# Small DMAs issued by GpSimd, and the SSD group norm spread as rows through DRAM

## The chip, the cores and the metric

One core of a Trainium2 chip runs the whole program. The metric is the device time of one execution in microseconds; lower is better. The core has five engines with a queue of instructions each: TensorE (PE), VectorE (DVE), ScalarE (ACT), GpSimd (POOL) and SyncE (SP). An engine takes its queue in order; semaphores tie the queues together.

## The reference

A decoder trunk of two layers on x of 512 tokens by 1024 channels, in float32. Each layer:

```python
u = rmsnorm(h); proj = u @ w_in              # D_IN columns for three branches and the gates
y_gla = group_rmsnorm(gla(q, k, v, decay), 4 groups) * silu(gg)
y_m   = group_rmsnorm(mlstm(q, k, v, i, f), 4 groups) * sigmoid(mo)
y = ssd(x, dt, a, b, c) + d * x              # 16 heads in 2 groups, chunked scan
y = y * silu(sz)
y_s   = group_rmsnorm(y, ssd_norm, 2 groups) # mean of squares over 512 channels, per token
z = [y_gla, y_m, y_s] @ w_branch             # one 1024 x 1024 product each
h += (sum of sigmoid(gates) * z) @ w_out
h += conv_ffn(rmsnorm(h))                    # 2816 wide, gated, causal conv of width 3
```

`group_rmsnorm(y)` divides each token's 512 channels of a group by the root of their mean square (plus 1e-6) and multiplies by a weight per channel.

## The kernel before

Activations lie with channels on the 128 partitions and the 512 tokens along the free axis, so a tile of 128 x 512 is one eighth of the model's width. Products are made in three parts from float32 split into a high and a low part (`wh`, `wl` for weights, `uh`/`ul`, `yh`/`yl`, `ah`/`al` for activations): each output tile of 128 channels takes 24 matmuls of 128 x 512 for an input of 8 tiles. Weights stream from DRAM in 512 KB pieces into three raw buffers, ACT rounds a piece to `wh`, DVE makes `wl`, and two chunks of split weights are held. Outputs go to four PSUM accumulators (`acc`), which DVE or ACT evacuates; smaller products use four other PSUM banks (`m`). Work tiles come from one pool of 37 buffers of 128 x 512 (`t`).

Order of a layer: the small columns and the SSD inputs; GLA's q, k, v; the SSD gate z (`sz`); the SSD branch product (two pairs of gate outputs come first, `SSD_AHEAD`); the mLSTM inputs; GLA's gate and branch; the mLSTM gate and branch; the output product; the FFN. Beside this foreground run generators in the background (`Bg`): the three sequence mixers and the norms. After each output tile the foreground calls `after_unit`, which splits the next weights and lets each generator go one step. The final order in each engine's queue is fixed before the run by a planner, which weighs the order of writing (some parts are raised with `high_priority`) against its own estimate of when things are ready.

All DMAs are issued by SyncE. The big ones are weights (`load`, L271 and L267). The small ones go through `self.dq` (L151):

- `rows` (L588 to L596) writes the per-head rows of decays to a DRAM tile `dr` and reads one of them back spread over partitions.
- `bcast` (L500) reads one row from DRAM into all 128 partitions, 256 KB. The SSD loop `mixes` in `ssd_group` uses it for each head's decay and two half-height ones (`eb`, L844 and L845) for each pair of heads; `mlstm_head` uses it twice for each head.
- `norm_rows` (L741) is the group norm of GLA and mLSTM: the sums of squares lie as rows, one root for all heads, four writes to a DRAM tile `dn` (L760) and a broadcast for each head.
- `emq` (L1016) and `wa` (L877).

The SSD group norm is `fin_s` (L927), once for each of two groups. The z evacuations square y and add the squares of a group's four tiles in `sqs[g]`. One background step later (`SQY`) `colsum` multiplies each block of 128 tokens, as weights, with a column of ones; the sums then lie as columns, 128 tokens on the partitions by 4 blocks. `rsqrt` makes the inverse root on this 128 x 4 tile by a bit trick and three Newton steps (ten small DVE operations with the first). At the next step `rows_of_cols` spreads it with four transposes into one PSUM tile that holds each token's value on all partitions, and the four y tiles of the group are scaled (L238 by the name `y<-y,par,m`) and split into `yh` and `yl`. The branch product starts once both groups are written out:

```python
def colsum(self, ps, o, q):
    for b in range(NB):
        self.mm(ps[:, o + b:o + b + 1], q[:, b * P:(b + 1) * P], self.ones[:, 0:1])
```

`sums` (L690), which GLA and mLSTM heads use, does the same with the roles turned: 32 columns of ones are the weights, the block of squares streams, and block b's result goes to partitions 32b to 32b + 31, so four matmuls run on four strips of 32 columns of the array.

In `branch`, the pair of outputs that meets the norm first is made in the order: first output on input tiles 0 to 6, second output on tiles 0 to 3, first output on tile 7, second output on tiles 4 to 7. Tiles 0 to 3 are of group 0, 4 to 7 of group 1.

Of the kernel before, what the change touches and what calls it, by code (L numbers as in the profile page):

```python
# [9 lines left out]
F32 = mybir.dt.float32  # L10
# [3 lines left out]
ALU = mybir.AluOpType  # L14
# [3 lines left out]
P = 128  # L18
L = 2
D = 1024  # L20
T = 512
KT = D // P
NB = T // P
EPS = 1e-6
# [74 lines left out]
class Bg:  # L99


    def __init__(self):
        self.g = []
# [30 lines left out]
class Kern:  # L134
    def __init__(self, ctx, tc, xT, w8, w11, par, wa, cst, out):
        self.tc, self.nc = tc, tc.nc
        nc = self.nc
        self.out = out
        self.w8, self.w11 = w8, w11
        pool = lambda name, bufs, **k: ctx.enter_context(tc.tile_pool(name=name, bufs=bufs, **k))  # L140
        self.pc = pool("pc", 1)
        self.ph = pool("ph", 1)
        self.pw = pool("pw", 2)
        self.pt = pool("pt", T_BUFS)
        self.pv = pool("pv", 8)
        self.ps = pool("ps", 1)
        self.pacc = pool("pacc", 4, space=PSUM)
        self.pm = pool("pm", 4, space=PSUM)
        self.pd = pool("pd", 2, space=DRAM)
        self.n = 0  # L150
        self.dq = nc.sync  # L151
        self.wide = False
        self.cst = self.pc.tile([P, NCST], F32, name="cst")
        self.cst_in, self.par_in = cst, par
        c = self.cst
        self.ident = c[:, 0:128]
        self.ones = c[:, 128:256]
        self.neg4 = c[:, 256:384].unsqueeze(1).to_broadcast([P, NB, P])
        self.scanmask = c[:, 512:1024]
        self.sgn = c[:, CST["sgn"]:CST["sgn"] + 1]  # L160
        self.mrow = c[:, CST["mrow"]:CST["mrow"] + 1]
        self.srow = c[:, CST["srow"]:CST["srow"] + 1]
        self.tri4f = c[:, 384:512].unsqueeze(1).to_broadcast([P, NB, P])
        self.tri4 = c[:, 384:512].bitcast(I32).unsqueeze(1).to_broadcast([P, NB, P])
        self.wa_in = wa
        self.pars = []
        for l in range(L):
            self.pars.append(self.pc.tile([P, NPAR], F32, name=f"par{l}"))
        self.par = self.pars[0]
        self.h = [None] * KT  # L170
        self.xT = xT
        self.kept = xT
        self.sct = [self.pc.tile([P, NB, P], F32, name=f"sct{i}") for i in range(2)]
        for s in self.sct:
            nc.gpsimd.memset(s, 0.0)
        self.nsct = 0
        self.bg = Bg()

        self.chunks = []
        for l in range(L):  # L180
            i = 0
            while i < NMIX:
                if i in TOK:
                    self.chunks += [(2, l * N8 + i, k, 2) for k in range(2)]
                    i += 4
                    continue
                n = 1 if i == NSSD - 1 else 2
                self.chunks.append((0, l * N8 + i, KT, n))
                i += n
            for half in range(2):  # L190
                for i in FFN_UP[half]:
                    self.chunks.append((0, l * N8 + NMIX + 2 * i, KT, 2))
                for i in range(KT):
                    self.chunks.append((1, (l * 2 + half) * KT + i, HALF, 1))
        self.cc = 0
        self.raw_q = []
        self.load_at = [0, 0]
        self.prep_at = [0, 0]
        self.split = {}
# [672 lines left out]
    def layer(self, l):  # L872
        nc = self.nc
# [51 lines left out]
        sqs, ready, ys, done_s = [None, None], [], [], []  # L925

        def fin_s(g):  # L927
            while g not in ready:
                yield
            for _ in range(SQY):  # L930
                yield
            ps = self.mps()
            self.colsum(ps, 0, sqs[g])
            var, r = self.small([P, NB], "svar"), self.small([P, NB], "sr")
            nc.vector.tensor_scalar(var, ps[:, 0:NB], 1.0 / 512, 4 * EPS, op0=ALU.mult, op1=ALU.add)
            with self.tc.high_priority(EV_PRIO):
                self.rsqrt(r, var, self.small([P, NB], "srt"))
            yield
            rr = self.rows_of_cols(r)
            for j in range(4 * g, 4 * g + 4):  # L940
                y = self.sy[j]
                self.stt(y, y, self.col("sn", j), rr, ALU.mult, ALU.mult)
                ys.append(self.split_tile(y))
                self.sy[j] = None
                if j % 2:
                    yield
            if g == 1:
                done_s.append(ys)
        bg.add(fin_s(0))
        bg.add(fin_s(1))  # L950
        for g in range(2):
            for i in range(2):
# [397 lines left out]
```

## Time and profile before

| | |
|---|---|
| median of 3 runs | 2295.11 us (2294.96 to 2295.38) |
| the profiled execution | 2295.16 us, span of its instructions 2293.3 us |
| granted TensorE clock | 0.998 of full speed |
| TensorE busy | 2279.3 us |
| DVE, ACT busy | 1434.1, 902.7 us |
| DMA | 235.73 MB, mean 103 GB/s |

The profiled execution differs from the median by 0.05 us. A matmul of 128 x 512 appears with about 0.39 us, but they are pipelined: in a stream one starts every 0.23 us, so costs on TensorE are read from one start to another, not from durations. A float32 product that is not split into parts appears as two instructions. The trace has no DMA issued by GpSimd, and its 22 instructions are memsets.

### The profile page before, as it was taken

The page shows a single profiled execution, that of the slowest core. Times are in us where ns is not written, and L with a number is a line of the kernel's source. Part 1 is how long each engine was busy: PE and PEld are TensorE (multiplying, and loading weights), DVE is VectorE, ACT ScalarE, POOL GpSimd, SP SyncE. Part 2 cuts the span into 40 slices and gives each one's busy share as a digit, 9 for nine tenths or more (in the row PEclk, how much of TensorE's full clock was granted, in tenths as well). Part 3 has the DMA queues.
Part 4 walks back from the last instruction along what each step waited for, and adds up shares of the span by engine and source line. Part 5 has one row for each costly group of instructions (what it writes and reads, how often), then busy time and mean ns, then how long its engine had stood idle before and what let it go on. Part 6 is the DMA issues. An engine that isn't in the chain of part 4 may idle for free.

```text
span 2293.3 us, 27258 instructions
## 1 busy us (share of the span) xinstructions
PE 2279.3 (99%) x10832; PEld 1876.8 (82%) x10832; DVE 1434.1 (63%) x2165; ACT 902.7 (39%) x1344; POOL 2.8 (0%) x22
## 2 busy tenths in 40 slices
PE   9999999999999999999999999999999999999998
PEld 6878888888888888888888788888888888888887
DVE  6966745474464587467579767345744645873774
ACT  6534632333333344234354346233333433442432
POOL 0000000000000000000000000000000000000000
PEclk9999999999999999999999999999999999999999
DMA  5253223332232333232323522232322343232222
GB/s 181 85 156 101 74 74 104 99 120 93 87 111 97 129 100 107 82 101 97 128 85 102 162 92 74 77 107 93 129 90 90 101 132 107 93 97 94 94 91 75
DMA packets 78911, 235.73 MB, mean 103 GB/s; under 512 B 8872, under 2 KB 12264, under 8 KB 78784
## 3 DMA queue, kind: packets, MB, share of 16 engines
q1 hardware_dynamic: 78784, 233.99, 31.7%
q8 instruction: 85, 1.39, 0.3%
q14 instruction: 42, 0.34, 0.1%
HBM read 229.55 MB, written 4.41 MB: 102 GB/s over the span
## 4 chain that ended last, share of the span: by engine, by line
PE 93%; DVE 4%; ACT 2%; issue 1%; DMA 1%; SPq 0%; DVEq 0%; ACTq 0%
PE acc L241 65%; PE m L241 27%; DVE cc L238 1%; PE m L244 1%; ACT la L229 1%; DVE wl L232 1%; DVE la L610 0%; DMA h<-in_xT 0%; DVE og L232 0%; DVE cx L232 0%; DMA dn<-ry 0%; ACT zg L229 0%; ACT cc L229 0%; DVE zg L238 0%; ACT wh L229 0%
## 5 line engine op out<-in xcount | busy, mean ns | idle before, releaser
L229 ACT ACTIVATE wh<-raw 128x1024 fp32r<-128x1024 f32 (+2 forms) x372 | 385.1, 1077 | 586.1 <-PE acc L241 250.9
L241 PE MATMUL acc<-uh,wh 128*128 128x512 f32 x1552 | 609.3, 393 | 2.0 <-DVE mo L232 1.0
L241 PE MATMUL acc<-uh,wl 128*128 128x512 f32 x1552 | 605.9, 391 | 0.4 <-DVE wl L232 0.3
L241 PE MATMUL acc<-ul,wh 128*128 128x512 f32 x1552 | 605.7, 390 | 0.1
L232 DVE TENSOR_TENSOR wl<-raw,wh 128x1024 fp32r<-128x1024 f32 (+2 forms) x372 | 453.2, 1250 | 154.4 <-ACT wh L229 154.0
L241 PEld LDWEIGHTS acc<-uh,wh 128*128 128x128 f32 x1552 | 291.4, 188 | 64.2 <-issue 2.7
L241 PEld LDWEIGHTS acc<-uh,wl 128*128 128x128 f32 x1552 | 291.4, 188 | 62.7 <-DVE wl L232 1.5
L241 PEld LDWEIGHTS acc<-ul,wh 128*128 128x128 f32 x1552 | 291.4, 188 | 61.6 <-DVE ul L238 1.6
L238 DVE SCALAR_TENSOR_TENSOR cc<-cx,par,cc 128x510 f32<-128x510 f32 (+2 forms) x296 | 217.6, 748 | 41.0 <-ACT cc L229 36.9
L241 PE MATMUL acc<-yl,wh 128*128 128x512 f32 x512 | 200.0, 391 | 0.0
L241 PE MATMUL acc<-yh,wl 128*128 128x512 f32 x512 | 199.7, 390 | 0.0
L241 PE MATMUL acc<-yh,wh 128*128 128x512 f32 x512 | 199.6, 392 | 0.0
L241 PE MATMUL m<-uh,wh 128*128 128x512 f32 x384 | 149.8, 390 | 1.2 <-ACT wh L229 1.2
L241 PE MATMUL m<-uh,wl 128*128 128x512 f32 x384 | 149.9, 390 | 0.0
L241 PE MATMUL m<-ul,wh 128*128 128x512 f32 x384 | 149.4, 389 | 0.0
L229 ACT ACTIVATE cc<-cx,par 128x512 f32<-128x512 f32 x128 | 102.8, 809 | 86.6 <-DVE cx L232 86.5
L241 PE MATMUL m<-ah,wl 128*128 128x512 f32 x308 | 120.0, 390 | 0.0
L241 PE MATMUL m<-al,wh 128*128 128x512 f32 x308 | 119.8, 389 | 0.0
L241 PE MATMUL m<-ah,wh 128*128 128x512 f32 x308 | 119.5, 389 | 0.0
L241 PEld LDWEIGHTS acc<-yh,wl 128*128 128x128 f32 x512 | 96.1, 188 | 20.5 <-issue 0.4
L241 PEld LDWEIGHTS acc<-yh,wh 128*128 128x128 f32 x512 | 96.1, 188 | 19.8 <-DVE gg L232 0.4
L241 PEld LDWEIGHTS acc<-yl,wh 128*128 128x128 f32 x512 | 96.2, 188 | 19.5
(204 smaller groups left out, 2653.3 us busy)
## 6 DMA issues: line engine op xcount, KB each, us to landing
raw<-in_w SPq DMA_DIRECT2D x336, 512.0 KB, 3.6
raw<-in_w SPq DMA_DIRECT2D x32, 704.0 KB, 4.0
bc<-dr SPq DMA_DIRECT2D x48, 256.0 KB, 3.6
h<-in_xT SPq DMA_DIRECT2D x16, 256.0 KB, 6.6
eb<-dr SPq DMA_DIRECT2D x32, 128.0 KB, 4.5
bc<-dn SPq DMA_DIRECT2D x16, 256.0 KB, 3.1
kept<-h SPq DMA_DIRECT2D x8, 256.0 KB, 2.0
h<-kept SPq DMA_DIRECT2D x8, 256.0 KB, 5.6
```

The costliest lines, as they stand in the source:

```text
L229: return self.nc.scalar.activation(out, in_, func, bias=bias, scale=scale)
L232: return self.nc.vector.tensor_tensor(out, a, b, op=op)
L238: return self.nc.vector.scalar_tensor_tensor(out, a, s, b, op0=op0, op1=op1)
L241: return self.nc.tensor.matmul(out, lhsT, rhs, start=start, stop=stop)
L244: return self.nc.tensor.transpose(out, x, self.ident)
```

## The change

`self.dq` becomes the GpSimd queue, so every small DMA named above is issued by GpSimd; weights, inputs, the kept residual and the output stay with SyncE. In `fin_s`, `colsum` gives way to `sums`; the inverse root is made on 128 x 128 (single buffers); the four strips' first rows are written to a DRAM tile `ds`, one row of 512 tokens, and `bcast` reads it back to all partitions into a work tile.

```diff
-        self.dq = nc.sync
+        self.dq = nc.gpsimd
...
             ps = self.mps()
-            self.colsum(ps, 0, sqs[g])
-            var, r = self.small([P, NB], "svar"), self.small([P, NB], "sr")
-            nc.vector.tensor_scalar(var, ps[:, 0:NB], 1.0 / 512, 4 * EPS, op0=ALU.mult, op1=ALU.add)
+            self.sums(ps, sqs[g])
+            var, r, s = (self.small([P, P], n, 1) for n in ("svar", "sr", "srt"))
+            nc.vector.tensor_scalar(var, ps[:, 0:P], 1.0 / 512, 4 * EPS, op0=ALU.mult, op1=ALU.add)
             with self.tc.high_priority(EV_PRIO):
-                self.rsqrt(r, var, self.small([P, NB], "srt"))
+                self.rsqrt(r, var, s)
+            ds = self.pd.tile([1, T], F32, name=f"ds_{self.n}", tag="ds")
+            self.n += 1
+            for b in range(NB):
+                self.dq.dma_start(ds[0:1, b * P:(b + 1) * P], r[32 * b:32 * b + 1])
+            rr = self.bcast(ds[0:1])
             yield
-            rr = self.rows_of_cols(r)
             for j in range(4 * g, 4 * g + 4):
```

## Rows read from the trace of the kernel before

**Rows 1.** The page's busy line: busy us, share of span, instructions of each engine.
```profile
PE 2279.3 (99%) x10832; PEld 1876.8 (82%) x10832; DVE 1434.1 (63%) x2165; ACT 902.7 (39%) x1344; POOL 2.8 (0%) x22
```
**Rows 2.** Windows, 18 to 2276 us: length, then each engine's busy us, clock, DMA.
```profile
18.00:2276.00 2258.00, 2256.11 (x10728) 1861.35 (x10728) 1414.06 (x2116) 887.45 (x1319) 1.64 (x16) 1.00 0.32 101
```
**Rows 3.** Timeline of TensorE, group 0's norm: start us, us, instruction.
```profile
239.25 0.95 PE L241 MATMUL m<-cst,sq 128*128 128x1 f32 x8
240.05 1.54 PE L241 MATMUL m<-v,kt 128*128 128x256 f32 x6
...
254.15 0.60 PE L244 MATMUL m<-cst,sr 128*128 128x128 f32 x4
254.59 0.61 PE L241 MATMUL m<-sct,v 128*128 128x128 f32 x4
```
**Rows 4.** Timeline of TensorE around one call of sums.
```profile
313.15 0.39 PE L241 MATMUL acc<-uh,wl 128*128 128x512 f32 x1
...
314.16 0.39 PE L241 MATMUL acc<-ul,wh 128*128 128x512 f32 x1
```
**Rows 5.** Timeline of DVE, group 1's norm in layer 1.
```profile
281.76 0.15 DVE L238 SCALAR_TENSOR_TENSOR sr<-srt,sr 128x4 f32<-128x4 f32 x1
...
287.28 2.72 DVE L238 SCALAR_TENSOR_TENSOR y<-y,par,m 128x512 f32<-128x512 f32 x4 [1.56 <-PE m L244]
289.92 2.36 DVE L232 TENSOR_TENSOR wl<-raw,wh 128x1024 fp32r<-128x1024 f32 x2
292.19 0.69 DVE L232 TENSOR_TENSOR yl<-y,yh 128x512 fp32r<-128x512 f32 x1
```
**Rows 6.** By tile, ry: count, duration ns min/median/max, first and last start, shapes.
```profile
L232 DVE TENSOR_TENSOR nt<-rx,ry x12: 685/692/694, 463.1 to 1766.0; 128x512 f32<-128x512 f32 x12
...
L474 DVE TENSOR_SCALAR ry<-rx x4: 415/419/421, 461.7 to 1760.1; 128x512 int32<-128x512 int32 x4
```
**Rows 7.** By tile, dr: issue durations ns, and time to landing.
```profile
L844 SPq DMA_DIRECT2D eb<-dr x16: 450/451/1820, 132.8 to 1314.7; - x16
...
L592 SPq DMA_DIRECT2D dr<-ig x2: 240/240/240, 77.4 to 1211.4; - x2
...
DMA to landing us min/median/max: 3.1/4.3/6.4
```
**Rows 8.** Timeline of SyncE's DMA issues, the mLSTM norm of layer 1.
```profile
633.72 1.21 SPq L760 DMA_DIRECT2D dn<-ry  x2
635.02 0.39 SPq L271 DMA_DIRECT2D raw<-in_w  x1
...
636.57 0.58 SPq L760 DMA_DIRECT2D dn<-ry  x1
640.82 1.75 SPq L502 DMA_DIRECT2D bc<-dn  x4
```
**Rows 9.** Timeline of DVE and of TensorE behind it; idle time and releaser in brackets.
```profile
643.91 2.50 DVE L232 TENSOR_TENSOR og<-og,bc 128x512 f32<-128x512 f32 x4 [7.29 <-DMA bc<-dn]
...
655.45 0.47 PE L241 MATMUL acc<-uh,wh 128*128 128x512 f32 x1 [0.98 <-DVE mo L232]
```
**Rows 10.** Timeline of TensorE in the SSD branch product of layer 1.
```profile
292.63 0.39 PE L241 MATMUL acc<-yh,wh 128*128 128x512 f32 x1
...
294.54 0.43 PE L241 MATMUL m<-sqo,cst 128*32 128x128 f32 x8
...
297.67 0.58 PE L241 MATMUL acc<-yl,wh 128*128 128x512 f32 x1
```
**Rows 11.** Timeline of GpSimd.
```profile
295.73 0.10 POOL L979 MEMSET v<- 128x4 f32 x1 [14.35 <-PE m L241]
```
**Rows 12.** Waits of SyncE's DMA queue: us in total, times, longest.
```profile
SPq L271 <- DVE wl L232: 1641.3, 313, 19.1
```
**Rows 13.** Timeline of DVE and TensorE in the SSD loop of layer 1.
```profile
157.95 0.68 DVE L232 TENSOR_TENSOR bc<-bc,cbt 128x512 f32<-128x512 f32 x1
...
158.80 0.43 PE L241 MATMUL m<-bc,xd 128*64 128x128 f32 x2
```

## The prediction

> **What bounds the kernel now.** I read the busy line of the page first: TensorE is busy 99% of the span, no other engine over 63%, GpSimd 2.8 us in all [rows 1]. Then the stretches: between 18 and 2276 us TensorE is idle for 2258.00 - 2256.11 = 1.9 us in total [rows 2]; the rest of its idle time is the first loads and the last norm, which the change doesn't touch. The chain of waits says the same, matmul after matmul. So a time can change in three ways only: TensorE gets less to do, one of the waits inside those 1.9 us goes, or a new wait appears because an operand comes late. Transfers and SyncE's queue count only through the last two.
>
> The profiled execution took 2295.16 us for a span of 2293.3; the median of the runs is 2295.11, so sums on the trace can be put against 2295.1.
>
> **TensorE's work in the group norms.** It exists four times (two groups, two layers). Removed are the sums in columns: eight instructions, 239.25 to 240.05, 0.80 us, with nothing lost at their ends; and the four transposes that spread the result, 254.15 to 254.59, 0.44 us [rows 3]. Added is one call of `sums`, which the GLA heads already make. One of these stands alone among projection matmuls: the last matmul before it starts at 313.15, the second behind it at 314.16 [rows 4]. Starts that would be 2 x 0.23 us apart in the stream are 1.01 us apart, so the call costs 1.01 - 0.46 = 0.55 us, the turn to the narrow tiles and back included. Each group gains 0.80 + 0.44 - 0.55 = 0.69 us, four groups 2.8 us. TensorE has no idle time there to swallow this, so all of it counts. If the narrow sums land beside another narrow call they share the turn, which is worth 0.1 to 0.2 us each; I leave that out.
>
> **The longer way of the norm's result.** Before, in group 1 of layer 1, the last operation of DVE's inverse root starts at 281.76 and ends at 281.91, and DVE starts scaling y at 287.28, once the transposes are through [rows 5]. After:
> - The root works on 128 x 128 instead of 128 x 4. An operation takes 0.15 us on 4 columns [rows 5] and 0.69 on 512 [rows 6], so about 0.29 on 128: 0.13 us more on each of ten, 1.3 us. It ends at 283.2. DVE has idle time behind it (1.56 us just before 287.28), so this costs latency and no more.
> - Four writes of a row to DRAM, issued one behind the other. No DMA is issued by GpSimd in this trace. By SyncE's issues of moved DMAs: the shortest is 0.24 us, the longest 1.82 [rows 7]; the nearest, the same write in the other norms (`dn`), is 0.58 [rows 8]. I take 4 x 0.58 = 2.3 (1.0 to 7.3).
> - From the end of the last write's issue to the broadcast that waits for it: 637.15 to 640.82, 3.7 us [rows 8]. From the broadcast's issue to the DVE operation that waits for it: 640.82 to 643.91, 3.1 us [rows 8, 9]; landings of the moved reads reach 6.4 [rows 7].
>
> Sum: 283.2 + 2.3 + 3.7 + 3.1 = 292.3, that is 5.0 us after 287.28 (3.7 with the shortest issues, 13.3 with the longest issues and landing). Group 0 goes the same way 30 us ahead of its use, so that its lateness is hidden by the z projections; group 1 has no such cover. The branch projection uses y tiles 0 to 3 (group 0) in its first twelve products and reaches tile 4 at 292.63 [rows 10], while the low half of tile 4 is made at 292.19 to 292.88 [rows 5]: no slack at all. What can cover the 5.0 us: the second output's twelve products on tiles 0 to 3 (12 x 0.227 = 2.7 us), the GLA pieces that now stand at 294.54 to 297.67 (3.1 us) [rows 10], and on DVE the two weight splits at 289.92, 2.3 us, which now delay the low half and could run during the wait [rows 5]. That is 5.8 us of TensorE work and 2.3 us of DVE work against 5.0, and another gate projection (48 products, 10.9 us) behind it. The order on each engine is fixed by the planner before the run; the sum of 2.8 us holds if it draws this work forward. I take that as likeliest, with a loss of nothing.
>
> The GpSimd queue has its own waiting instructions: eight memsets of v tiles in each layer, each waiting for a TensorE matmul. Group 1's writes (ready at 283.2) stand ahead of the one at 295.73 in order of time [rows 11], and then it costs nothing; behind it they would be 12 us late, which is rival B below, made worse. That y is scaled by a tile in SBUF, not in PSUM, frees a PSUM bank and takes one more of the 37 work buffers; I count neither.
>
> **The moved queue.** 136 DMAs leave SyncE (layer rows, 64 broadcasts of 256 KB, 32 of 128 KB, `dn`, `emq`, `wa`) and go to GpSimd with 20 new ones. SyncE's weight loads wait 1641 us in total for DVE to free a buffer [rows 12], and whatever is queued behind one waits with it. But TensorE doesn't wait for weights: of its 1.9 us one wait of 0.98 us is tied to a small DMA. There the four `dn` writes are issued from 633.72 to 637.15, with two weight loads between them, DVE then stands 7.29 us before the broadcast lands with finished accumulators behind it, and TensorE runs out of accumulators at 655.45 [rows 8, 9]. Without the loads between, 4 x 0.58 = 2.3 us in place of 3.43, this wait goes (-1.0 us); with issues of 1.82 us the four take 7.3, and TensorE waits 3.9 us longer in each layer (+7.7). The nearest row (0.58) gives the -1.0, but it needs landings as short as SyncE's too, which no row shows; so I take 0 for the move, leave the -1.0 to rival D and keep both ends for the range.
>
> **Forecast**: 2295.2 - 2.8 = 2292.4 us, by itself 2290.5 to 2295.
>
> **The Trainium skill on GpSimd's DMAs.** The trace shows the integer scalar operation of the root on 128x512 in 0.42 us where a two-input operation takes 0.69 [rows 6], so DVE has a faster way through single-input fp32 work. The Trainium skill (SBUF — State Buffer, SBUF: two separate sides) warns that while DVE runs in such a two-port mode GpSimd can't write the descriptors of a DMA, and advises SyncE or ScalarE as the issuer. That speaks against the move, most of all in the SSD stage, where four scalar operations go with every broadcast; by it each DMA could be held for one such operation, and rival C below is where this would show. The Trainium skill (DMA: Bandwidth & Descriptors, Specifications) also gives a first byte of about 1 us from GpSimd against 0.6 from SyncE: an estimate of 2 x 0.4 = 0.8 us more in the norm's way, 5.8 in place of 5.0. No run here shows either yet.
>
> **Rivals.**
> - B, slower: the planner keeps the order of before and group 1 comes late. TensorE then reaches tile 4 at 292.63 less 2 x 0.69, at 291.3, and waits until 292.88 + 5.0 = 297.9: 6.6 us in each layer. 2295.2 - 2.8 + 13.2 = 2305.6; with the two weight splits drawn ahead of the scaling 2301.0; with the longest issues 2322. It decides from the point where the lateness exceeds what is drawn forward. For it: in the `dn` chain the planner did put work that needs a landed broadcast ahead of ready evacuations, and DVE stood 7.29 us [rows 9]. Against it: in the same stage it already mixes GLA pieces into the branch products [rows 10].
> - C, slower: the SSD loop. Its broadcasts are used at once: DVE ends the masked decay at 158.63 and TensorE starts the product at 158.80 [rows 13]. There are 16 such sets. If a GpSimd issue makes the second broadcast of a set 0.5 us later and the order is the old one, TensorE waits up to 16 x 0.5 = 8 us: 2300.4. Below 0.17 us of delay it costs nothing. Against it: buffers and other projections leave the planner free to place sets earlier.
> - D, faster: with the small DMAs free, the remaining waits of TensorE (1.9 us) go too, and the SSD products, now cut by turns between 64-wide and full tiles, are ordered better: 2295.2 - 2.8 - 1.9 - 1 = 2289.5. For it: the one DMA wait of 0.98 us. Against it: the other waits have DVE's order behind them.
> - E: the change does nothing that counts, because the moved DMAs were hidden and the planner's new order gives back the 2.8 us in turns between tile widths: 2295.
>
> **Chances.** The forecast 0.40, B 0.22, C 0.10, D 0.22, E 0.06. About 0.2% (4.6 us) is what a measurement of this kernel can tell from no change. D is beyond it in nearly all its outcomes and the forecast's low end touches it: faster 0.24. B and most of C are beyond it on the other side: slower 0.29. Within: 0.47. The range runs from 2288 to 2306, leaving out B's long issues and a D with more than the waits.
>
> **What would show it.** Right: 16 fewer transposes, 32 fewer one-column products and 32 more narrow sums in the list of matmuls, TensorE's busy time 2.8 us lower, its idle time between 18 and 2276 us still about 2 us. B: a TensorE wait of several us at the fourth tile of the SSD branch, once in each layer, released by a low half of y or the broadcast of `ds`. C: waits before the SSD products, released by DVE's masked decay. D: no TensorE wait near 655 us. The prediction is wrong if TensorE's idle time in the SSD and norm stages grows beyond 3 us, or if GpSimd's issues take much over 0.6 us and this reaches TensorE.

## The result, and the profile after

The changed kernel takes 2317.89 us (median), the kernel before 2295.24 on the same chip: a ratio of 1.0097, interval 1.008 to 1.0115. It is 1% slower, 25 us above the forecast and outside its range. The profiled execution has 2317.57 us and a span of 2315.8.

The busy line of the page, and the window from 18 to 2276 us, of the changed kernel:

```profile
PE 2285.8 (99%) x10816; PEld 1877.1 (81%) x10816; DVE 1438.1 (62%) x2165; ACT 901.8 (39%) x1344; POOL 85.2 (4%) x178
```
```profile
18.00:2276.00 2258.00, 2240.64 (x10571) 1839.61 (x10570) 1410.52 (x2107) 881.63 (x1312) 83.39 (x171) 1.00 0.32 102
```

TensorE has the 16 instructions less that were to go, but is busy 6.5 us longer than in [rows 1]. Its idle time in the window is 2258.00 - 2240.64 = 17.4 us, against 1.9 in [rows 2]. The waits of TensorE in the changed kernel (us in total, times, longest) name who came late. Of the five longest, four are at the mLSTM norms and at the SSD norm and branch; the one for `wh` is at the kernel's start, where there were waits before too:

```profile
PE acc L241 <- DVE mo L232: 4.6, 2, 2.5
PE acc L241 <- DVE G L232: 2.8, 2, 1.4
PE acc L241 <- DVE sz L232: 2.2, 2, 1.1
PE acc L241 <- ACT wh L229: 2.1, 1, 2.1
PE acc L241 <- DVE yl L232: 1.9, 1, 1.9
```

The 9234 wide matmuls (those with `wh` or `wl`) come in nearly one order of work (in the changed kernel 150 of the 9234 places hold another product than before, in e4 481), so I laid the start of the n-th one of each trace beside that of before. The growth of the difference in six stages, in us (worked out from the starts; numbers of the matmuls in brackets), for all runs. Each row is one execution; that of e2 is 1.6 us under the median of its runs:

```
                          SSD    SSD norm,  mLSTM   SSD    SSD norm,  mLSTM
                          loop   branch     norm    loop   branch     norm
                          L1     L1         L1      L2     L2         L2     span
                         (300-  (720-      (2370-  (5040-  (5280-    (6380-
                          720)   1110)      2520)   5280)   5660)     7100)
changed kernel            1.2    4.3        2.7     1.7     7.7       4.4    22.5
e1_queue_only             1.6   -0.0        1.3     1.7     0.0       5.0    10.4
e2_norm_only              0.0    4.8        0.4    -0.0     3.7       0.5     9.3
e3_no_round_trip          1.1   -1.1        1.4     1.7    -1.0       5.5     7.8
e4_ahead3                 1.1    1.9        1.3     1.7     0.8       6.6    14.8
e5_no_trip_sync           0.1   -1.1        0.9    -0.0    -1.1       0.5    -1.3
e6_norm_gpsimd            0.4    6.1        0.3     0.0     4.5       0.5    12.5
e7_norm_gpsimd_ahead3     0.0    2.5       -0.5    -0.0     1.4       1.8     5.7
e8_before_ahead3          0.0    0.0       -0.4    -0.0     0.0       0.7     0.3
e9_queue_split            1.1   -0.0        0.8     1.7     0.0       2.2     6.9
e10_norm_sqy0             0.3    9.3        0.7     0.0     8.6       0.2    18.7
e11_norm_ahead3           0.7    0.1       -0.6    -0.0    -0.5       0.7     0.8
e12_norm_sqy0_ahead3      0.9    6.8        0.5     0.0     4.5       1.0    13.9
e13_dn_gpsimd             0.4    0.0       -0.5    -0.0     0.0       0.3     0.2
e14_ssd_gpsimd            1.2   -0.0       -0.6     1.7     0.0       0.5     2.8
e15_norm_ahead4          -0.0    0.1        0.6    -0.0    -0.5       0.7     1.5
e16_emq_gpsimd            0.1   -0.0        0.8    -0.0     0.0       2.0     3.2
e17_queue_no_emq          1.1   -0.0       -0.8     1.7     0.0       0.1     2.6
e18_dn_emq_gpsimd         0.1    0.0        1.7    -0.0     0.0       2.8     4.6
```

Three places lose time: the SSD loops, the SSD norms with the branch behind them, and the mLSTM norms (the last column takes in the GLA gate of layer 2). Differences of up to 1.0 us at the mLSTM norms, in e7 1.8, also occur in kernels that change nothing there, so a single entry of that size says little. In e4, e7, e11, e12 and e15 another 0.6 us follows right behind the SSD norm's stage of layer 2, up to matmul 5800.

**The SSD norm.** VectorE's timeline in the changed kernel, group 1 of layer 1 (idle time and its releaser in brackets), and the start of the same root before:

```profile
284.69 0.29 DVE L935 TENSOR_SCALAR svar<-m 128x128 f32<-128x128 f32 x1 [1.19 <-PE m L241]
284.90 1.22 DVE L232 TENSOR_TENSOR wl<-raw,wh 128x1024 fp32r<-128x1024 f32 x1
...
291.96 0.29 DVE L238 SCALAR_TENSOR_TENSOR sr<-srt,sr 128x128 f32<-128x128 f32 x1
...
299.55 2.74 DVE L238 SCALAR_TENSOR_TENSOR y<-y,par,bc 128x512 f32<-128x512 f32 x4 [3.24 <-DMA bc<-ds]
```
```profile
279.30 0.16 DVE L935 TENSOR_SCALAR svar<-m 128x4 f32<-128x4 f32 x1 [2.80 <-PE m L241]
```

The scaling is 299.55 - 287.28 = 12.3 us later than in [rows 5]. Its three legs: the root starts 5.4 us later; it takes 284.69 to 292.25 = 7.6 us where it took 279.30 to 281.91 = 2.6 (its operations have the 0.29 us that was estimated, but weight splits, key and query products and state updates stand between them); and from the root to the scaling 7.3 us go by where 5.4 did. About 1 us of the 12.3 comes from the SSD loop, behind which the whole stream of TensorE is that much later. On GpSimd's timeline the four writes take 1.92 us and the broadcast follows:

```profile
292.55 1.92 POOL L941 DMA_DIRECT2D ds<-sr  x4 [6.01 <-DVE sr L238]
296.13 0.58 POOL L502 DMA_DIRECT2D bc<-ds  x1 [1.66 <-ACT gdec L229]
299.75 0.10 POOL L983 MEMSET v<- 128x4 f32 x1 [3.04 <-PE m L241]
```

The memset of [rows 11] stands behind them. TensorE's waits around this branch, where [rows 10] had none:

```profile
278.20 0.50 PE L241 MATMUL acc<-uh,wh 128*128 128x512 f32 x1 [1.11 <-DVE sz L232]
...
291.19 0.71 PE L241 MATMUL m<-sct,v 128*128 128x128 f32 x4 [0.56 <-DVE st L238]
295.30 0.50 PE L241 MATMUL acc<-yh,wh 128*128 128x512 f32 x1 [1.39 <-DVE G L232]
```

None of these three waits is for y: what came late are other operations of VectorE (`sz`, `st`, `G`), whose order around the norm is a new one. Only layer 2 has a long wait for a low half of y:

```profile
1447.15 0.50 PE L241 MATMUL acc<-yl,wh 128*128 128x512 f32 x1 [1.90 <-DVE yl L232]
```

**The mLSTM norm.** VectorE and, from the last row, TensorE in the changed kernel, layer 1, beside [rows 8, 9]:

```profile
639.39 1.23 DVE L232 TENSOR_TENSOR wl<-raw,wh 128x1024 fp32r<-128x1024 f32 x1 [0.70 <-ACT wh L229]
640.53 0.68 DVE L238 SCALAR_TENSOR_TENSOR ry<-nt,ry 128x512 f32<-128x512 f32 x1
...
650.76 1.29 DVE L232 TENSOR_TENSOR og<-og,bc 128x512 f32<-128x512 f32 x2 [7.80 <-DMA bc<-dn]
...
662.29 0.47 PE L241 MATMUL acc<-uh,wh 128*128 128x512 f32 x1 [2.10 <-DVE mo L232]
```

The last step of the root (`ry`) now stands behind a weight split that waits for ScalarE. The way from its end to the landed broadcast is 641.21 to 650.76 = 9.6 us, no longer than before (633.69 to 643.91 = 10.2).

### The profile page after: what moved, and what is told of

It reads as the page before. It is cut to its first block, busy times and chain, and to the rows that moved or that the text cites. A ratio compares the mean times of both kernels' runs of the same rounds, so it can differ in the third digit from the quotient of the medians.

```text
span 2315.8 us, 27332 instructions
## 1 busy us (share of the span) xinstructions
PE 2285.8 (99%) x10816; PEld 1877.1 (81%) x10816; DVE 1438.1 (62%) x2165; ACT 901.8 (39%) x1344; POOL 85.2 (4%) x178
## 3 DMA queue, kind: packets, MB, share of 16 engines
q8 instruction: 85, 1.39, 0.2%
## 4 chain that ended last, share of the span: by engine, by line
PE 92%; DVE 4%; issue 2%; DMA 2%; ACT 1%; POOL 0%; SPq 0%; DVEq 0%; POOLq 0%; ACTq 0%
PE acc L241 64%; PE m L241 27%; PE m L244 1%; DVE og L232 1%; DVE wl L232 1%; DMA bc<-dn 0%; DMA dn<-ry 0%; ACT la L229 0%; DMA bc<-ds 0%; DVE yl L232 0%; DVE cc L238 0%; DMA raw<-in_w 0%; ACT wh L229 0%; DMA bc<-dr 0%; POOL dn L760 0%
```

## The experiments

Theory N put the loss on the norm's longer way, theory Q on the queue.

**e1, the queue alone** (the kernel before with the small DMAs on GpSimd).

```
-        self.dq = nc.sync
+        self.dq = nc.gpsimd
```

> The kernel before with the small DMAs on GpSimd's queue, the group norm as it was. Theory N (the norm's longer way is the cause): of the 22.7 us between the two kernels, about 14 lie at the two SSD norms and branches, and they are not here; what may stay is the mLSTM norms, the GLA gate and the SSD loop of the second layer, 0 to 8 us: 2295 to 2303 us. Theory Q (the queue is the cause, the landings come later everywhere): 2310 to 2318 us, with TensorE waits at the mLSTM norms (near 655 and 1805 us) and in the SSD loop.

2305.22 us, ratio 1.0046 (1.0031 to 1.0061). Between the two theories: the queue costs 10.3 us, and none of it at the SSD norms.

**e2, the norm alone** (the changed kernel with `self.dq = nc.sync`).

> The changed kernel with all small DMAs back on SyncE's queue, the norm's own four writes and its broadcast too. Theory N: the 14 us at the SSD norms stay, or grow, since the writes now stand behind weight loads: 2308 to 2325 us. Theory Q: the loss goes with the queue, and the 2.8 us of TensorE's work remain won: 2292 to 2297 us.

2306.11 us, ratio 1.0047 (1.0032 to 1.0062). The norm costs 11.2 us, at its own place. 10.3 + 11.2 = 21.5 of the 22.7: the two parts add up within their intervals (some 3 us each way), and each theory was half the truth.

**e3, no round trip.**

```
-            rr = self.bcast(ds[0:1])
+            rr = self.bcast(self.dr[4 * g:4 * g + 1])
```

> The changed kernel, but y is scaled by a broadcast of a layer row that is in DRAM from the start, not by the root just made; the sums, the root and its four writes are still made (the value that scales y is another one). So the chain from sums to scaling is cut, and nothing else is taken away. If the lateness of the norm's result is what costs: the 14 us at the two SSD norms go, 2302 to 2306 us. If it is the new order on VectorE and ScalarE whatever the lateness: 2313 to 2319 us. If the queue is the cause (theory Q): 2313 to 2318 us as well, and the two are told apart by the run with the queue alone.

2303.96 us, ratio 1.0038 (1.0023 to 1.0053). The SSD norm stages go from +4.3 and +7.7 to -1.1 and -1.0 us. So the loss there hangs on the trip from the root to the scaling, and what is left is the queue's. The edit also lets the planner lay these stages anew (TensorE's order differs from the changed kernel's in some 30 places), so this run doesn't tell the wait itself from the order that the planner makes for it. Like e5 below, the kernel leaves out the norm: y is scaled by another row.

**e4, more cover** (`SSD_AHEAD = 3`).

> The changed kernel with SSD_AHEAD 3 in place of 2: the SSD branch stands one more gate projection (48 products, about 11 us of TensorE) behind the norm. If the lateness of the norm's result costs because too little TensorE work covers it: some 10 of the 14 us come back, 2303 to 2310 us. If the order on VectorE and ScalarE or the queue is the cause: 2314 to 2320 us. A later branch can also move its evacuations into the next stage and cost there; then above 2320 us.

2309.65 us, ratio 1.006 (1.0043 to 1.0077): 8.2 us back, from the SSD norm stages.

**e5, e3's edit in e2's kernel.**

> Norm changed as in the run with the norm alone (all DMAs on SyncE), but y scaled by a layer row that is in DRAM from the start, as in the run without the round trip (the root and its writes are made, the value that scales y is another one). The runs so far add up: the queue +10.3, the norm +11.2, and 2.4 us won at the norms where the trip is cut. By that sum this kernel has the 2.8 us of TensorE's work as its only difference: 2292 to 2294 us, the SSD norm stages 1.2 us shorter in each layer. If the later norms suffer from the norm's order whatever the trip: 2297 to 2300 us.

2293.67 us, ratio 0.999 (0.9981 to 1.0), as the sum said. TensorE is busy 2277.6 us, 1.7 less than before, with 16 instructions less, and each SSD norm stage is 1.1 us shorter. This is what the new sums are worth if nothing waits for them, and even this is under the 0.2% that can be told from no change.

**e6, only the norm's own DMAs on GpSimd** (e2 with `self.dq = nc.gpsimd` around the four writes and the broadcast).

> All small DMAs on SyncE except the new norm's own twenty, which GpSimd issues with nothing else in its queue. If SyncE's weight loads hold up the norm's writes in the run with the norm alone (2306.1 us), this is faster: 2298 to 2303 us. If GpSimd's longer landings count for more: 2306 to 2312 us, with 4 and 7.5 us lost in the two SSD norm stages as in the changed kernel. Elsewhere (SSD loop, mLSTM norms) no loss by either.

2308.10 us, ratio 1.0056 (1.0041 to 1.0071): GpSimd is no quicker way. On its queue a write of `ds` is issued in 484 to 614 ns, and 7.2 us pass from the root's end (291.25) to the scaling (298.45). On SyncE's, in e2, it is 240 to 253 ns, and 5.3 us pass (both rows below are of e2):

```profile
289.38 0.29 DVE L238 SCALAR_TENSOR_TENSOR sr<-srt,sr 128x128 f32<-128x128 f32 x1
...
294.92 2.74 DVE L238 SCALAR_TENSOR_TENSOR y<-y,par,bc 128x512 f32<-128x512 f32 x4 [2.03 <-DMA bc<-ds]
```

**e7, e6 with `SSD_AHEAD = 3`.**

> The kernel above with SSD_AHEAD 3. In the changed kernel that gave back 7.6 us of 22.7. If more TensorE work between the norm and the branch covers the round trip: 2296 to 2300 us (the run with both less the queue's 10.3 is 2299.3). If it covers it in full: 2292 to 2294 us, faster than before. If the GLA gate of the second layer is late by the later branch (3 us there in the run with both): 2300 to 2303 us.

2300.93 us, ratio 1.0024 (1.0015 to 1.0033): 7.2 us back, not all.

**e8, the control** (before with `SSD_AHEAD = 3`).

> The kernel before with SSD_AHEAD 3, nothing else: the control for the later branch. If the later branch has no price of its own: 2294 to 2296 us. If it has (buffers held longer, evacuations moved into the next stage): 2297 to 2301 us, and that much of the runs with SSD_AHEAD 3 is not the norm's.

2295.32 us, ratio 0.9999 (0.9989 to 1.0008). The later branch has no price of its own.

**e9, the queue without the norms' DMAs** (e1 with `dn` and its broadcasts on SyncE).

> The queue alone once more, but the writes and broadcasts of the GLA and mLSTM norms (`dn`, 24 of the DMAs in each layer) stay on SyncE. With the queue alone 3.2 us went at the two SSD loops (10 and 4 more turns between tile widths, no wait) and 6.0 at the two mLSTM norms. If each stage's loss comes from its own DMAs: 2298 to 2299.5 us, TensorE's order in the SSD loops as with the queue alone, the mLSTM norms as before. If the mLSTM norms are late from what happened before them: 2303 to 2306 us.

2302.17 us, ratio 1.0033 (1.0021 to 1.0044), between the two. Some 3 us remain at the mLSTM norms though their DMAs are where they were.

**e10, the sums one step earlier** (e2 with `SQY = 0`).

> The norm alone (all DMAs on SyncE) with SQY 0 in place of 1: the sums are put into the program one step earlier. In the run with the norm alone the trip through DRAM takes 5.3 us from the root's end to the scaling, as the way through the transposes did (281.91 to 287.28), so the lateness comes from the sums (282.05 on TensorE, 278.32 before) and the root (289.66, 281.91 before). If that is so and the earlier step moves the sums up by some 3 us: 2299 to 2303 us. If the planner places them by its own clock: 2305 to 2307 us. If the order around them gets worse: above 2308 us.

2314.97 us, ratio 1.0089 (1.0072 to 1.0106): the worst end. The sums start earlier (281.17 for 282.05) and so does the scaling (292.98 for 294.92), and still the stages lose 9.3 and 8.6 us, since another order comes with it: TensorE has 12 products of the branch ahead of those that need group 1, where e2 has 24, and waits for y 1.81 us at 294.45. So the hour of the scaling alone doesn't set the loss, but how much work the order has left for TensorE at that moment. Not all of the 9.3 us is waiting: the granted clock of 295 to 302 us is 0.51 (the lower level, 1.2 GHz, in nearly all of it). Wide matmuls there start 0.43 us apart (298.17, 298.60, 299.03) and not 0.23, so an estimate is 2.6 us of the 5.64 in which TensorE is busy:

```profile
295.00:302.00 7.00, 5.64 (x18) 4.79 (x19) 7.00 (x14) 4.76 (x13) 0.00 (x0) 0.51 0.00 0
```

**e11, e2 with `SSD_AHEAD = 3`.**

> The norm alone on SyncE with SSD_AHEAD 3. The later branch by itself costs nothing (2295.3 us without the change). With the norm's DMAs on GpSimd it was 2300.9 us, and SyncE was 2.0 us better with SSD_AHEAD 2. If more cover is all that is needed: 2292 to 2295 us. If half the loss stays, since VectorE still stands in order for the broadcast: 2297 to 2300 us.

2295.78 us, ratio 1.0002 (0.9992 to 1.0011). With 48 products more between the norm and its use, the loss of the norm is gone within the interval. What the sums win is spent at TensorE's waits for the gate:

```profile
PE acc L241 <- DVE G L232: 2.8, 2, 1.4
```

**e12, e10 and e11 together.**

> Both: SQY 0 and SSD_AHEAD 3, the norm alone on SyncE. The candidate for a version that beats both: if earlier sums and more cover add up, 2292 to 2295 us; if the norm's order costs whatever the cover, 2297 to 2301 us.

2308.10 us, ratio 1.0058 (1.0043 to 1.0073). The bad order costs more than the cover gives.

**e13, the norms' DMAs alone on GpSimd** (before, with `self.dq = nc.gpsimd` around `dn` and its broadcasts).

> The kernel before with the writes and broadcasts of the GLA and mLSTM norms alone on GpSimd; all else as before. In the run with the queue alone 6.0 us went at the mLSTM norms, in the one that leaves these DMAs on SyncE 2.6. If they make the difference: 2297.5 to 2299 us, all of it near 655 and 1790 us. If the mLSTM norms are late by what came before them: 2294.5 to 2296 us.

2295.09 us, ratio 1.0 (0.9991 to 1.0009). They cost nothing by themselves.

**e14, the SSD loops' broadcasts alone on GpSimd.**

```
-                e = self.bcast(dr[16 + hd:17 + hd])
+                e = self.t("bc")
+                nc.gpsimd.dma_start(e, dr[16 + hd:17 + hd].partition_broadcast(P))
...
-            self.dq.dma_start(e2[0:64], dr[32 + hd:33 + hd].partition_broadcast(64))
+            nc.gpsimd.dma_start(e2[0:64], dr[32 + hd:33 + hd].partition_broadcast(64))
...
```

> The kernel before with the 64 broadcasts of the SSD loops alone on GpSimd (32 of 256 KB, 32 of 128 KB). If these make TensorE's order in the SSD loops worse: 50 and 22 turns between widths in place of 40 and 18, 3.2 us, 2297.5 to 2299 us, without a TensorE wait. If the other moved DMAs (layer rows, the GLA and mLSTM heads' broadcasts) do: 2294.5 to 2296 us.

2298.43 us, ratio 1.0012 (1.0003 to 1.0021): 3.1 us, at the SSD loops. The windows of its two loops (length, busy time of TensorE first), and the same two before:

```profile
80.00:205.00 125.00, 125.00 (x658) 98.54 (x658) 98.03 (x225) 45.40 (x71) 17.35 (x32) 1.00 0.41 127
1270.00:1340.00 70.00, 70.00 (x406) 55.59 (x405) 48.83 (x114) 23.40 (x39) 12.88 (x24) 1.00 0.49 146
```
```profile
80.00:205.00 125.00, 125.00 (x663) 99.36 (x663) 98.12 (x226) 45.86 (x73) 0.00 (x0) 1.00 0.42 129
1270.00:1340.00 70.00, 70.00 (x414) 56.88 (x413) 47.62 (x110) 23.85 (x40) 0.00 (x0) 1.00 0.46 144
```

TensorE has no idle time there, and gets 658 and 406 instructions done where it did 663 and 414. It goes 48 and 22 times between wide and narrow products in the two loops, before 40 and 18. This is order, not waiting.

**e15, e2 with `SSD_AHEAD = 4`.**

> The norm alone on SyncE with SSD_AHEAD 4: twice the cover of SSD_AHEAD 3, with which it was 2295.8 us against 2295.1. If the TensorE waits left there (2.8 us for VectorE's gate products) come from the broadcast and go with more cover: 2292 to 2294 us, faster than both. If they come from the order that the norm brings: 2295 to 2298 us.

2295.41 us, ratio 1.0002 (0.9993 to 1.0011), with the same 2.8 us of waits for `G`. More cover wins nothing more.

**e16, `emq` alone on GpSimd** (before, four DMAs in each layer).

```
-            self.dq.dma_start(emq[32 * b:32 * b + 32].rearrange("p (h t) -> p h t", h=4),
+            nc.gpsimd.dma_start(emq[32 * b:32 * b + 32].rearrange("p (h t) -> p h t", h=4),
```

> The kernel before with the four `emq` DMAs of each layer alone on GpSimd. In the two runs that lost time at the mLSTM norms, VectorE's last Newton step (`ry`) stands behind a weight split that waits for ScalarE, 2.0 us late; in the two that lost nothing there it stands ahead of it. With `emq` alone moved it stands behind, and all else of VectorE's order is the same. If that order is the cause: each mLSTM norm 1 to 2 us longer, 2297 to 2299 us, with a TensorE wait for `mo`. If it is the later landings of the norms' DMAs: 2294.5 to 2296 us.

2299.03 us, ratio 1.0018 (1.0008 to 1.0027): 3.9 us. On TensorE and ScalarE the order is that of before; on VectorE one weight split in each layer changes places with `ry`. Its timeline, with TensorE's wait in the last row:

```profile
633.47 1.23 DVE L232 TENSOR_TENSOR wl<-raw,wh 128x1024 fp32r<-128x1024 f32 x1 [0.70 <-ACT wh L229]
634.62 0.68 DVE L238 SCALAR_TENSOR_TENSOR ry<-nt,ry 128x512 f32<-128x512 f32 x1
...
644.56 2.50 DVE L232 TENSOR_TENSOR og<-og,bc 128x512 f32<-128x512 f32 x4 [7.52 <-DMA bc<-dn]
...
656.10 0.47 PE L241 MATMUL acc<-uh,wh 128*128 128x512 f32 x1 [1.81 <-DVE mo L232]
```

**e17, the queue without `emq`** (e1 with `nc.sync` there).

> The queue alone (2305.2 us) with the `emq` DMAs back on SyncE: TensorE's order is the same, and the last Newton step stands ahead of the weight split again. If that step's place is the cause of the 6.0 us at the mLSTM norms: 3.2 us (the SSD loops) are left, 2298 to 2299.5 us. If the landings of the norms' broadcasts on GpSimd are: 2303 to 2305 us.

2297.63 us, ratio 1.0013 (1.0003 to 1.0022). Eight DMAs put back give 7.6 of the 10.3 us; TensorE's and ScalarE's order is that of e1, and on VectorE `ry` stands ahead of the split again. The same places:

```profile
634.62 0.69 DVE L238 SCALAR_TENSOR_TENSOR ry<-nt,ry 128x512 f32<-128x512 f32 x1
635.28 2.36 DVE L232 TENSOR_TENSOR wl<-raw,wh 128x1024 fp32r<-128x1024 f32 x2
...
644.72 1.29 DVE L232 TENSOR_TENSOR og<-og,bc 128x512 f32<-128x512 f32 x2 [6.47 <-DMA bc<-dn]
...
656.25 0.47 PE L241 MATMUL acc<-uh,wh 128*128 128x512 f32 x1 [0.17 <-DVE mo L232]
```

The mLSTM wait of [rows 9] is 0.17 us here, in place of 0.98. That is what rival D said of the move, but it isn't shown: in e11 and e14, where the norms' DMAs stay on SyncE, the same wait is 0.38 and 0.41 us.

**e18, `emq` and the norms' DMAs on GpSimd.**

> The kernel before with `emq` and the norms' writes and broadcasts on GpSimd, the rest on SyncE. Each alone: the norms' DMAs cost nothing (2295.1 us); `emq` is in the run beside. If the late step and the later landing add up beyond what TensorE's accumulators cover, this has the 6.0 us at the mLSTM norms that the whole queue has: 2299 to 2302 us. If they don't: as `emq` alone.

2300.78 us, ratio 1.0024 (1.0013 to 1.0034): 5.6 us, though the norms' DMAs alone cost nothing and `emq` alone 3.9. With the step late, TensorE's accumulators run out anyway, and then the later landing counts too: the wait for `mo` in layer 1 is 2.69 us, with `emq` alone 1.81.

So the 22.7 us are: 11.2 for the norm's late result, 3.1 for the SSD loops' order, 5.6 for the swapped step with the later landings behind it. The remaining 2.8 us have no run of their own, and stay open; each part's interval is about as wide (2 to 3.5 us each way). No version beat the kernel before by a measurable amount.

## Why the prediction was wrong, step by step

- **What bounds the kernel**: right. TensorE was always busy, and the change could only bring waits or turns. The sign that was named for being wrong came: over 3 us of idle time of TensorE in these stages (17.4 us in the window).
- **TensorE's work, -2.8 us**: right in kind, somewhat smaller in size. Cut from the trip (e5), it is 2.2 us in the two SSD stages and 1.8 in all.
- **"It ends at 283.2"**: the step that failed first. The root ends at 292.25. I added the length of ten operations to the old start, and took the order around them as given; but the planner laid the whole stretch anew, the sums behind the projection's end and weight splits between the root's steps. Some 9 us of the lateness come from there.
- **The trip of 9.1 us**: too long. It took 7.3 on GpSimd and 5.3 on SyncE, and the way through the transposes had taken 5.4. On GpSimd the four issues took 1.92 us (2.3 taken), the broadcast followed the last of them by 1.7 (3.7 taken) and landed 3.4 later (3.1 taken). In the sum 283.2 + 9.1 = 292.3 a leg too long hid a little of the leg too short.
- **"The sum of 2.8 us holds if it draws this work forward. I take that as likeliest, with a loss of nothing"**: wrong, and the costliest choice. The pieces of GLA work that I counted as cover were placed ahead of the branch (in e2 from 282.29 to 284.97) and were gone when y was late. The second output's twelve products were drawn forward as counted (295.30 to 297.97 in the changed kernel), but only after 1.39 us of waiting for `G`, VectorE's evacuation of an accumulator. What this cost, measured alone, is the 11.2 us of e2. On SyncE one gate projection more is cover enough (e11), on GpSimd it is not (e7). Rival B put the price of the norm alone at 2305.6; e2 measured 2306.1, but that the numbers meet is luck: its waits in layer 1 are 1.4 us for `G`, 1.0 for `yh` and 1.2 for `ge`, not 6.6 at the fourth tile.
- **The memsets on GpSimd's queue**: right, the writes stand ahead.
- **"So I take 0 for the move"**: wrong by 10.3 us. The bounds -1.0 to +7.7 were worked out for the norms' own landings, and these alone cost 0 (e13), as taken. The cost came by two ways that I hadn't asked about: the order of the SSD loops, which rival C priced at up to 2300.4 as waits and which came as turns (e14: 2298.4, so C's number is near by luck), and a step of VectorE that changed places with a weight split because four other DMAs left SyncE's queue (e16, e17).
- **The chances**: the forecast, B and C were weighed as alternatives. They lie at different places and each can happen without the others, so their prices add: B's 13.2 us and C's 8 on 2292.4 give 2313.6. The range should have reached there, and even that is short of the 2317.9 measured.
- **The Trainium skill**: the rule that VectorE's two-port mode keeps GpSimd from writing descriptors (SBUF — State Buffer, SBUF: two separate sides) shows in no issue time here. GpSimd's issues in the SSD loops, beside the scalar operations, stayed short (count, ns min/median/max):

```profile
L502 POOL DMA_DIRECT2D bc<-dr x48: 536/541/572, 129.0 to 1737.0; - x48
L844 POOL DMA_DIRECT2D eb<-dr x16: 530/530/542, 133.3 to 1323.4; - x16
```

against 450 to 1820 for L844 in [rows 7]. Whether the rule was put to the test is open, because I took the faster mode from operations on 128x512 [rows 6]. The scalar operations of the SSD loops (L837) take 283 ns in the changed kernel, as long as a two-input one on the same shape:

```profile
L837 DVE TENSOR_SCALAR bc<-bc,ca 128x128 f32<-128x128 f32 x128 | 27.9, 283 | 12.2 <-DMA bc<-dr 11.8
L232 DVE TENSOR_TENSOR srt<-svar,sr 128x128 f32<-128x128 f32 x12 | 3.4, 286 | 0.1
```

The Trainium skill's later first byte from GpSimd, by 0.4 us (DMA: Bandwidth & Descriptors, Specifications), agrees as far as landings can tell: the first broadcast of each set of `dn` landed 3.4 to 3.8 us after its issue by GpSimd, and 3.1 to 3.3 by SyncE before.
- **SyncE's weight loads** wait even longer for VectorE, 1842.5 us against 1641.3 in [rows 12], and it still cost nothing:

```profile
SPq L271 <- DVE wl L232: 1842.5, 324, 31.6
```

## What to carry to other kernels

Where a planner fixes the order of each engine, a change of queue or latency can be a change of order on other engines (e14, e16), though not every such move costs time (e13): compare the orders around the critical stages, not only the moved instructions. Latency is free only as far as work that can run is still placed behind it; one constant (here `SSD_AHEAD`) can show in one run whether cover is what lacks. And rivals at different places are not alternatives: add their prices before setting the range.

## What was not expected of the hardware

More time can go at a wait of TensorE than its length. In the changed kernel, after the 2.10 us wait that ends at 662.29, matmuls that start 0.23 us apart start 0.43 us apart for seven in a row; the granted clock of 663 to 667 us is 0.57 (the lower level, 1.2 GHz, in most of it), and 1.00 right after:

```profile
663.00:667.00 4.00, 4.00 (x12) 3.11 (x12) 4.00 (x6) 1.20 (x3) 0.00 (x0) 0.57 0.24 45
667.00:671.00 4.00, 4.00 (x19) 3.32 (x18) 3.01 (x5) 1.88 (x4) 0.00 (x0) 1.00 0.59 217
```

Seven times 0.20 us is 1.4 us on top of the 2.1. The same comes once more in this kernel, in the SSD branch of layer 2 behind the 1.90 us wait for `yl` that ends at 1447.15, and in e10 (above):

```profile
1448.00:1452.00 4.00, 4.00 (x13) 3.16 (x12) 2.83 (x6) 3.29 (x6) 0.00 (x0) 0.57 0.00 0
```

By this estimate some 3 of the 6.5 us by which TensorE's busy time grew come from the clock, and with them part of the SSD norm's loss in layer 2. It doesn't follow every wait: in the same kernel the 2.54 us wait that ends at 1811.17 is followed by a granted clock of 1.00, as is the 0.98 us wait of [rows 9]; in the run with the queue alone the clock is 0.57 from 1797 to 1801, behind the longest wait for `mo`. What decides between them was not tried, and that the wait brings the lower clock is not shown.
